# A two-block transformer on one core: gathered rows, gate writes, convolution sums and class values rearranged in a TensorE-bound kernel

## Chip, core and metric

The kernel runs on one core of a Trainium2 chip. The metric is the device time of one execution in microseconds (us); less is better.

## What is computed

The input is one sequence of 512 tokens of 1024 values in fp32. Two blocks follow each other. The parts that the change touches are these, from the reference:

```python
# first block: convolution branch, and the expert layer
glu = zca * jax.nn.sigmoid(zcb)
cv = causal_depthwise_conv(glu, conv_w[l], conv_b[l])            # 31 taps
cv = jax.nn.silu(layer_norm(cv, conv_ln_g[l], conv_ln_b[l]))
y_b = cv @ w_b[l]
...
def block(args):                                                   # 128 experts a token (8 heads x 16)
    hb, eb, gb = args
    act = jax.nn.gelu(jnp.einsum('thkd,td->thk', u_tab[eb], hb), approximate=False)
    return jnp.einsum('thk,thkd->td', gb * act, v_tab[eb])
...
# second block: attention over blocks, and over tokens that lie 4 apart
for (win, dil, nh) in A_GROUPS:                                    # ((128,1,6), (512,4,5), (2048,16,5))
    ...
    v_sel = vg[:, idx]
    o = jnp.einsum('bqhk,bqkhd->bqhd', p.astype(vg.dtype), v_sel)
```

`u_tab` and `v_tab` have 16,384 rows of 1024 values. The second block also has a differential attention and two MLPs, which the change leaves alone.

## The kernel before

Activations lie with features on the 128 partitions and the 512 tokens along the free axis, in eight tiles. Every product is formed from a high and a low part, so each is three matmuls (L121, L122, L123 in `mm3`): high by high, high weight by low activation, low weight by high activation. Weights come as units of 128x1024 fp32 (0.524 MB). `unit` loads one into `raw` over SP's DMA queue (L94; three buffers), ScalarE (ACT) rounds it to `whi` (L103) and VectorE (DVE) makes the rest `wlo` (L104). A raw buffer is free again after L104. In the expert stage a fourth pair of whi and wlo buffers is used. The order of instructions on each engine is set when the kernel is built, by a scheduler that simulates a timeline; on the chip each engine and each DMA queue keeps to that order.

**Convolution sums (`stage_a`).** After the 31 taps the layer norm needs, for each token, the sum over all 1024 channels. The eight tiles `cv` are multiplied by a matrix of ones on TensorE (PE) and accumulated in PSUM (L346), the mean is subtracted (L351, DVE), the squares made on ACT (L353) and summed by eight more matmuls with ones (L354). An fp32 matmul with ones runs as two passes, so the trace has 16 for eight. At the same time the recurrent branch's output `O` is made tile by tile: PE transposes (L339), DVE gates the result (L340), ACT and DVE split it (L112, L113). The gemms with `w_a` consume `O` in the same order, three at a time (one for each of the three PSUM tiles `g`).

**Experts (`stage_p`).** 384 tokens are done densely: a loop of 32 chunks ("u loop") multiplies four units of `peer_u` each by the 384 tokens, applies gelu on ACT (L578) and writes the chunk `at` to DRAM (`act_d`, L579). Beside it `route` builds the gates: for 32 tokens at a time DVE makes one-hot tiles `oj`, `ol`, `oh` (L722 to L725), PE multiplies them (L730, L731), ACT copies the result into `G` (L733, 8 copies, one buffer) and SP writes the 2.1 MB of `G` to `g_d` (L736); that happens 12 times. The second loop of 32 chunks ("v loop") reads `at` back (L588) and the gates `gt` of that chunk (L589), which need all 12 writes; 0.786 MB each. DVE multiplies them to `w` (L591), ACT and DVE split it into `wph` and `wpl` (L112, L113), and PE adds 72 matmuls of 512 columns a chunk to six PSUM accumulators (L601 to L603). `prep(c + 1)` runs a chunk ahead.

The remaining 128 tokens are done by gathering table rows with an indirect DMA from POOL (GpSimd; L649): 128 gathers from `peer_ur` ("dots": DVE multiplies and reduces each, L654), then 128 from `peer_v` ("sums": DVE accumulates into `yt`, L664 and L666). Each gather moves 128 rows, 0.524 MB. Dots and sums form one generator, `gather_steps`, with four buffers `gu`; a call `gather(n)` advances it by n.

**Class values (`attn0`).** For the heads of the dilated groups the values are needed with tokens of one residue modulo 4 together. `vgemm_class` runs `gemm_tok` (L157 to L159) with N = 320 columns of weights moving; the stationary operand is an activation tile of which every fourth token is taken (`CLS`). That is 96 matmuls a call, and two calls. `cls_pv` multiplies the values `vC` with the transposed probabilities (L1065, L1066, L1072).

Of the kernel before, what the change touches and what calls it, by code (L numbers as in the profile page):

```python
# [52 lines left out]
class Kern:  # L53
# [188 lines left out]
    def stage_a(self):  # L242
# [33 lines left out]
        with self.pool("a_sl") as sl, self.pool("a_glu") as gl:  # L276
# [52 lines left out]
            with self.pool("a_tmp") as pt:  # L329
# [25 lines left out]
                va = tmp("mu", 1)  # L355
                nc.scalar.copy(out=va, in_=ps)
                vt = nps("m")
                for b in range(4):
                    nc.tensor.matmul(vt[:, 2 * b:2 * b + 2], va[:, self.BLK[b]], self.ident[:, 0:2], start=True, stop=True)
# [187 lines left out]
    def stage_p(self):  # L547
# [7 lines left out]
        with self.pool("p_gath") as pgt, self.pool("p_wh") as pwh, self.pool("p_wl") as pwl:  # L555
# [6 lines left out]
            steps = self.gather_steps(pgt)  # L562

            def gather(n):
                for _ in range(n):
                    next(steps, None)
            with self.pool("p_at") as pa, self.pool("p_rp", bufs=2, space=PSUM) as pq:
                self.route(pq, X, g_d, gather)
                TD = self.TD
                for c in range(CH):  # L570
                    at = pa.tile([P, 4, TD], F32, tag="at0", name="at0", bufs=2)
                    for i in range(4):
                        hi, lo = self.unit(A["peer_u"][c * 4 + i])
                        ps = self.pg.tile([P, T], F32, tag="g", name="g")[:, 0:TD]
                        for k in range(KD):
                            w = slice(k * P, (k + 1) * P)
                            self.mm3(ps, hi[:, w], lo[:, w], X[0][k][:, P:], X[1][k][:, P:], k == 0, k == KD - 1)
                        nc.scalar.activation(out=at[:, i], in_=ps, func=AF.Gelu)  # L578
                    nc.sync.dma_start(out=act_d[c], in_=at)  # L579
                    gather(1)  # L580
            with self.pool("p2") as pp, self.pool("p2p", space=PSUM) as pv:
                tmp = self.tmpf(pp, 2)
                acc = [self.pg.tile([P, T], F32, tag="g", name="g") if n < 3 else pv.tile([P, T], F32, name=f"ac{n}") for n in range(2 * ND)]

                def prep(c):
                    at = pp.tile([P, 4, TD], F32, tag="at", name="at", bufs=2)
                    gt = pp.tile([P, 4 * ND, 4, 32], F32, tag="gt", name="gt", bufs=2)
                    nc.sync.dma_start(out=at, in_=act_d[c])  # L588
# [15 lines left out]
                Ws = {0: prep(0)}  # L604
                for c in range(CH):
                    if c + 1 < CH:
                        Ws[c + 1] = prep(c + 1)
                    W = Ws.pop(c)
                    if c + 1 < CH:
                        for i in range(4):  # L610
                            hi, lo = self.unit(A["peer_v"][c * 4 + i])
                            for b in range(ND):
                                vmm(b, i, W, hi, lo, c == 0 and i == 0, False)
# [5 lines left out]
                    gather(6)  # L619
                gather(1000)  # L620
# [20 lines left out]
    def gather_steps(self, pool):  # L641


        nc, A = self.nc, self.A
        tabs = A["peer_ur"], A["peer_v"].rearrange("i j d -> (i j) d")

        def rows(tab, s):
            t = pool.tile([P, 1024], F32, tag="gu", name="gu", bufs=4)
            nc.gpsimd.indirect_dma_start(  # L649
                out=t, out_offset=None, in_=tab, in_offset=bass.IndirectOffsetOnAxis(ap=self.eidx[:, s:s + 1], axis=0))  # L650
            return t
        for s in range(P):
            u = rows(tabs[0], s)
# [6 lines left out]
            yield  # L660
        for s in range(P):
            v = rows(tabs[1], s)
# [305 lines left out]
    def attn0(self, X, g):  # L968
        nc, tc, A = self.nc, self.tc, self.A
        with self.pool("at0") as pa, self.pool("at0s") as ps_, self.pool("at0p", space=PSUM) as ppool:  # L970
# [5 lines left out]
            vC = [pa.tile([P, 4, 320], F32, name=f"vC{c}") for c in range(2)]  # L976
# [91 lines left out]
            def cls_pv(pr, po, pTs):  # L1068
                for r in range(4):
                    for hh in range(2):  # L1070
                        i = 2 * pr + hh - 6
                        nc.tensor.matmul(po[64 * hh:64 * hh + 64, self.BLK[r]], vC[i // 5][:, r, (i % 5) * 64:(i % 5) * 64 + 64], pTs[hh][:, self.BLK[r]],  # L1072
                                         start=True, stop=True)
# [8 lines left out]
            vgemm_class(0)  # L1082
            keep = {}
            for pr in range(3, 8):
# [7 lines left out]
                if pr < 5:  # L1092
                    po = pp("O")
# [43 lines left out]
            vgemm_class(1)  # L1137
# [216 lines left out]
def pack(I):  # L1354
# [37 lines left out]
    D["a_v1"] = _tok(w[:, 2432:3072], 320, 2)  # L1392
# [24 lines left out]
```

## Time and profile before

| what | value |
|---|---|
| time, median of 3 runs | 3213.58 us (3207.55 to 3220.32) |
| the profiled execution's own time | 3211.22 us |
| its span, first to last instruction | 3209.4 us |
| PE busy | 3072.0 us, 96% of the span |
| DVE busy | 2239.3 us, 70% |
| ACT busy | 1246.3 us, 39% |
| POOL busy | 420.3 us, 13% |
| DMA | 581.30 MB, mean 181 GB/s |
| mean granted TensorE clock | 0.984 of full speed |

The span runs from the first instruction to the last; the time of an execution is some 2 us longer. Busy times of consecutive matmuls overlap, since they are pipelined, so PE's pace is read as the count of matmuls in a stretch, and its idle time as what is missing from 50 us in a window of 50. A hole in PE's work counts where the last wait in it ends; idle time of another engine counts for nothing by itself.

### The profile page before, as it was taken

Reading aid. Unit: us, or ns where it says so; the run is one execution under the profiler, and the core shown is the slowest. Engines: PE = TensorE matmul, PEld = TensorE weight load, DVE = VectorE, ACT = ScalarE, POOL = GpSimd, SP = SyncE. Lnnn points to the kernel's source line nnn. Section 1 sums busy time; section 2 is a strip of 40 time slices with the busy share of each in tenths; the row PEclk is TensorE's granted clock in tenths of the full one; section 3 lists DMA queues with packets and bytes.
Section 4 is the critical chain, followed back from the end, with each engine's and each line's share of the span. In section 5 each row is a group of like instructions: output and inputs, shape, how many; then the busy total and the mean of one; then the engine's idle time right before and its main releaser. Section 6 shows DMA issues by size and latency. Waiting matters only on the chain.

```text
span 3209.4 us, 40754 instructions
## 1 busy us (share of the span) xinstructions
PE 3072.0 (96%) x15395; PEld 2604.1 (81%) x15395; DVE 2239.3 (70%) x4004; ACT 1246.3 (39%) x1970; POOL 420.3 (13%) x328
## 2 busy tenths in 40 slices
PE   6999999899999999599989999999999999999998
PEld 4788878789999899587777887788888877778886
DVE  7999967699999999787776545445544457554443
ACT  4267762334334343333223334453222245532221
POOL 0000000000333333444441001000000000000000
PEclk9999999999999999799999999999999999999999
DMA  6442227435899899999997642222333333133332
GB/s 220 147 165 70 73 86 234 152 101 158 310 340 357 323 360 345 375 361 354 342 330 265 229 147 88 62 65 81 105 97 94 110 92 96 51 96 97 97 99 72
DMA packets 200548, 581.30 MB, mean 181 GB/s; under 512 B 18368, under 2 KB 72528, under 8 KB 198816
## 3 DMA queue, kind: packets, MB, share of 16 engines
q1 hardware_dynamic: 160144, 432.93, 40.5%
q0 software_dynamic: 39776, 144.97, 12.1%
q8 instruction: 121, 1.98, 0.3%
q10 hardware_dynamic: 432, 0.80, 0.1%
q14 instruction: 75, 0.61, 0.1%
HBM read 526.12 MB, written 63.00 MB: 184 GB/s over the span
## 4 chain that ended last, share of the span: by engine, by line
PE 85%; DMA 6%; DVE 5%; issue 2%; ACT 2%; POOL 0%; DVEq 0%; POOLq 0%; SPq 0%; ACTq 0%
PE g L121 21%; PE g L122 20%; PE g L123 20%; DMA raw<-in_peer_v 4%; PE g L601 2%; PE g L602 2%; PE ac L601 2%; PE ac L602 2%; PE g L603 2%; PE ac L603 2%; PE S L1224 1%; DVE wlo L104 1%; PE L L480 1%; DVE yt L666 1%; PE Gp L730 1%
## 5 line engine op out<-in xcount | busy, mean ns | idle before, releaser
L103 ACT CAST whi<-raw 128x1024 fp32r<-128x1024 f32 (+2 forms) x556 | 577.0, 1045 | 1164.5 <-PE g L122 669.9
L121 PE MATMUL g<-xh,whi 128*128 128x512 f32 (+1 forms) x2368 | 874.0, 371 | 16.8 <-ACT xh L112 8.9
L123 PE MATMUL g<-xh,wlo 128*128 128x512 f32 (+1 forms) x2368 | 872.6, 370 | 6.6 <-DVE wlo L104 6.6
L122 PE MATMUL g<-xl,whi 128*128 128x512 f32 (+1 forms) x2368 | 875.8, 370 | 3.1 <-DVE xl L113 3.1
L104 DVE TENSOR_TENSOR wlo<-raw,whi 128x1024 fp32r<-128x1024 f32 (+2 forms) x556 | 674.5, 1215 | 220.1 <-ACT whi L103 216.6
L121 PEld LDWEIGHTS g<-xh,whi 128*128 128x128 f32 x2368 | 446.9, 189 | 77.3 <-ACT xh L112 9.3
L123 PEld LDWEIGHTS g<-xh,wlo 128*128 128x128 f32 x2368 | 446.6, 189 | 61.6 <-DVE wlo L104 8.1
L122 PEld LDWEIGHTS g<-xl,whi 128*128 128x128 f32 x2368 | 446.9, 189 | 59.8 <-DVE xl L113 5.3
L649 POOL DMA_INDIRECT gu<-in_peer_v,eidx x128 | 202.5, 1582 | 253.8 <-DVE yt L666 220.3
L649 POOL DMA_INDIRECT gu<-in_peer_ur,eidx x128 | 161.7, 1264 | 474.5 <-DVE ga L654 222.0
L601 PE MATMUL g<-whi,wph 128*128 128x512 f32 x384 | 155.4, 406 | 51.8 <-ACT whi L103 28.3
L121 PE MATMUL g<-mh,whi 128*128 128x512 f32 x512 | 199.2, 389 | 0.0
L122 PE MATMUL g<-ml,whi 128*128 128x512 f32 x512 | 199.2, 389 | 0.0
L123 PE MATMUL g<-mh,wlo 128*128 128x512 f32 x512 | 199.2, 389 | 0.0
L188 POOL TENSOR_TENSOR tr_r<-tr_v,mhalf 128x4 f32<-128x4 f32 x15 | 17.3, 1156 | 1281.9 <-DVE tr_v L187 1281.9
L914 DVE TENSOR_TENSOR h<-g,h 128x512 f32<-128x512 f32 x64 | 44.3, 692 | 194.0 <-PE g L123 194.0
L666 DVE SCALAR_TENSOR_TENSOR yt<-gu,ga,yt 128x1024 f32<-128x1024 f32 x127 | 163.1, 1284 | 20.0 <-DMA gu<-in_peer_v,eidx 18.8
L327 DVE SCALAR_TENSOR_TENSOR s<-glu,vec,s 128x512 f32<-128x512 f32 x232 | 164.3, 746 | 0.1
L654 DVE CUSTOM_DVE_ANT_0 gu<-gu,xt 128x1024 f32<-128x1024 f32 x128 | 155.4, 1220 | 6.1 <-DMA gu<-in_peer_ur,eidx 5.9
L602 PE MATMUL g<-whi,wpl 128*128 128x512 f32 x384 | 154.3, 402 | 0.0
L601 PE MATMUL ac<-whi,wph 128*128 128x512 f32 x384 | 153.1, 400 | 0.0
L602 PE MATMUL ac<-whi,wpl 128*128 128x512 f32 x384 | 152.3, 397 | 0.0
(443 smaller groups left out, 4750.8 us busy)
## 6 DMA issues: line engine op xcount, KB each, us to landing
raw<-in_peer_u SPq DMA_DIRECT2D x128, 512.0 KB
raw<-in_peer_v SPq DMA_DIRECT2D x128, 512.0 KB
raw<-in_mlp_in SPq DMA_DIRECT2D x64, 512.0 KB
raw<-in_mlp_out SPq DMA_DIRECT2D x64, 512.0 KB
raw<-in_w_in SPq DMA_DIRECT2D x56, 512.0 KB
act_d<-at SPq DMA_DIRECT2D x32, 768.0 KB
g_d<-G SPq DMA_DIRECT2D x12, 2048.0 KB
at<-act_d SPq DMA_DIRECT2D x32, 768.0 KB
```

Of the source, the lines that this page charges most:

```text
L103: nc.scalar.copy(out=hi[:, :n], in_=raw[:, :n])
L104: nc.vector.tensor_sub(out=lo[:, :n], in0=raw[:, :n], in1=hi[:, :n].bitcast(F32))
L121: nc.tensor.matmul(ps, wh, xh, start=start, stop=False)
L122: nc.tensor.matmul(ps, wh, xl, start=False, stop=False)
L123: nc.tensor.matmul(ps, wl, xh, start=False, stop=stop)
L327: nc.vector.scalar_tensor_tensor(o, glu[n][:, j:j + T], self.v("conv_w", n * 31 + j), acc, ALU.mult, ALU.add)
L601: nc.tensor.matmul(ps, wh[:, i], hi[:, s], start=first, stop=False)
L602: nc.tensor.matmul(ps, wl[:, i], hi[:, s], start=False, stop=False)
L603: nc.tensor.matmul(ps, wh[:, i], lo[:, s], start=False, stop=last)
L649: nc.gpsimd.indirect_dma_start(out=t, out_offset=None, in_=tab, in_offset=bass.IndirectOffsetOnAxis(ap=self.eidx[:, s:s + 1], axis=0))
L654: nc.vector.tensor_tensor_reduce(out=u, in0=u, in1=self.xt, scale=1.0, scalar=0.0, op0=ALU.mult, op1=ALU.add, accum_out=self.ga[:, s:s + 1])
L666: nc.vector.scalar_tensor_tensor(self.yt, v, self.ga[:, s:s + 1], self.yt, ALU.mult, ALU.add)
```

## The change

Four parts. **Gathers:** the generator is split. The dots have a pool of their own during `route` and the u loop and are drained at its end; the sums begin only in the v loop, in its pool, two ahead of the first chunk and then four and five a chunk by turns (six a chunk before, of whichever were left). **Chunk order:** the last u chunk's `at` is not written to DRAM and read back; the v loop begins with it and goes on with 0 to 30. The `at` tiles of both loops come from one pool. **Convolution sums:** DVE adds the eight tiles of `cv`, and one matmul with ones follows; the squares are added on DVE by `sq_add`, and the four small matmuls behind them multiply by ones in place of the identity. **Class values:** `vgemm_class` is called for each pair of heads (`pr` 3 to 7); it runs `gemm_unit` (24 matmuls of 512 columns, weights stationary), copies the result on ACT, transposes the four classes on PE and scales them on DVE into one tile `vC`. The weights are packed as units; their bytes are the same.

```diff
@@ stage_a
-                ps = nps("m")
-                for k in range(KD):
-                    nc.tensor.matmul(ps, self.ones, cv[k], start=(k == 0), stop=(k == KD - 1))
+                cs = tmp("mu", 1)
+                nc.vector.tensor_tensor(cs, cv[0], cv[1], ALU.add)
+                for k in range(2, KD):
+                    nc.vector.tensor_tensor(cs, cs, cv[k], ALU.add)
+                ps = nps("m")
+                nc.tensor.matmul(ps, self.ones, cs, start=True, stop=True)
                 mu = tmp("mu", 1)
                 nc.scalar.activation(out=mu, in_=ps, func=AF.Copy, scale=1.0 / 1024)
-                ps = nps("m")
+                va = tmp("va", 1)
                 for k in range(KD):
                     nc.vector.tensor_sub(cv[k], cv[k], mu)
-                    sq = tmp()
-                    nc.scalar.activation(out=sq, in_=cv[k], func=AF.Square)
-                    nc.tensor.matmul(ps, self.ones, sq, start=(k == 0), stop=(k == KD - 1))
-                va = tmp("mu", 1)
-                nc.scalar.copy(out=va, in_=ps)
+                    self.sq_add(tmp, va, cv[k], k == 0)
@@ stage_p
-            steps = self.gather_steps(pgt)
...
+            with self.pool("p_gu") as pgu, self.pool("p_rp", bufs=2, space=PSUM) as pq:
+                dots = self.gather_dots(pgu)
+                self.route(pq, X, g_d, lambda n: gather(dots, n))
                 for c in range(CH):
...
-                    nc.sync.dma_start(out=act_d[c], in_=at)
-                    gather(1)
+                    if c < CH - 1:
+                        nc.sync.dma_start(out=act_d[c], in_=at)
+                    gather(dots, 3 if c < 16 else 2)
+                gather(dots, 1000)
+                last = at
             with self.pool("p2") as pp, self.pool("p2p", space=PSUM) as pv:
+                sums = self.gather_sums(pp)
+                gather(sums, 2)
...
-                    nc.sync.dma_start(out=at, in_=act_d[c])
+                    if c < CH - 1:
+                        nc.sync.dma_start(out=at, in_=act_d[c])
...
-                for c in range(CH):
+                order = [CH - 1] + list(range(CH - 1))
+                Ws = {0: prep(order[0])}
+                for n, c in enumerate(order):
...
-                    gather(6)
-                gather(1000)
+                    gather(sums, 5 if n % 2 else 4)
+                gather(sums, 1000)
@@ attn0
-            def vgemm_class(c):
-                self.gemm_tok(pp, ("g", "g", "g", "T"), [A["a_v1"][c * 4 + i] for i in range(4)], 320, X,
-                              lambda b, ps: nc.scalar.activation(out=vC[c][:, b], in_=ps, func=AF.Copy, scale=self.rt[:, 4 + b:5 + b]),
-                              lambda b: self.CLS[b])
+            def vgemm_class(pr):
+                ps = self.gemm_unit(A["a_v1"][pr - 3], X)
+                v = tmp()
+                nc.scalar.copy(out=v, in_=ps)
+                tp = pp("T")
+                for r in range(4):
+                    nc.tensor.transpose(tp[:, self.BLK[r]], v[:, self.CLS[r]], self.ident)
+                c = (pr - 3) * P
+                nc.vector.tensor_tensor(
+                    vC[:, :, c:c + P], tp.rearrange("p (r d) -> p r d", r=4), self.rt[:, 4:8].unsqueeze(2).to_broadcast([P, 4, P]), ALU.mult)
...
-            vgemm_class(0)
...
                 if pr < 5:
+                    vgemm_class(pr)
                     po = pp("O")
...
-            vgemm_class(1)
+            for pr in range(5, 8):
+                vgemm_class(pr)
```

How the compiled order moves is shown at three places. Each row has its place on its engine, its line, the operation and the tiles.

First DVE at the convolution sums, where PE waits for DVE to make `O` (L340, then L113). Before:

```order
622 L528 SCALAR_TENSOR_TENSOR s_3010<-s_3010,s_2990,M 128x128 x2
623 L340 SCALAR_TENSOR_TENSOR s_415<-b,vec,s_3513 128x512
624 L340 SCALAR_TENSOR_TENSOR s_416<-b,vec,s_3524 128x512
625 L317 TENSOR_SCALAR ms<-ms 128x4
626 L113 TENSOR_TENSOR s_3521<-s_415,s_3505 128x512
627 L113 TENSOR_TENSOR s_3532<-s_416,s_3506 128x512
628 L320 TENSOR_TENSOR s_422<-s_422,ms 128x512
629 L340 SCALAR_TENSOR_TENSOR s_417<-b,vec,s_3535 128x512
```

After (L346 and L348 are now the adds of `cv`):

```order
622 L528 SCALAR_TENSOR_TENSOR s_3010<-s_3010,s_2990,M 128x128 x2
623 L346 TENSOR_TENSOR mu<-glu_439,glu_440 128x512
624 L348 TENSOR_TENSOR mu<-mu,glu_441 128x512
625 L348 TENSOR_TENSOR mu<-mu,glu_442 128x512
626 L348 TENSOR_TENSOR mu<-mu,glu_443 128x512
627 L340 SCALAR_TENSOR_TENSOR s_415<-b,vec,s_3513 128x512
628 L340 SCALAR_TENSOR_TENSOR s_416<-b,vec,s_3524 128x512
629 L348 TENSOR_TENSOR mu<-mu,glu_444 128x512
630 L317 TENSOR_SCALAR ms<-ms 128x4
631 L340 SCALAR_TENSOR_TENSOR s_417<-b,vec,s_3535 128x512
632 L113 TENSOR_TENSOR s_3521<-s_415,s_3505 128x512
```

Four adds now stand ahead of the first gated tile, and six instructions in place of three lie between its L340 and its L113.

Second SP's DMA queue from the last `peer_u` weights to the first gates read. Before:

```order
184 L736 DMA g_d<-G 128x4096
185 L579 DMA act_d<-at_12079 128x1536
186 L94 DMA raw<-in_peer_v 128x1024 x3
187 L579 DMA act_d<-at_12212 128x1536
188 L94 DMA raw<-in_peer_v 128x1024
189 L736 DMA g_d<-G 128x4096
190 L94 DMA raw<-in_peer_v 128x1024 x2
191 L736 DMA g_d<-G 128x4096
192 L588 DMA at<-act_d 128x1536
193 L589 DMA gt<-g_d 128x12x128
```

After (L749 is the write of `G`, L597 and L598 the reads of `at` and `gt`):

```order
186 L749 DMA g_d<-G 128x4096
187 L94 DMA raw<-in_peer_v 128x1024
188 L583 DMA act_d<-at 128x1536
189 L94 DMA raw<-in_peer_v 128x1024
190 L597 DMA at<-act_d 128x1536
191 L94 DMA raw<-in_peer_v 128x1024 x3
192 L749 DMA g_d<-G 128x4096
193 L94 DMA raw<-in_peer_v 128x1024
194 L749 DMA g_d<-G 128x4096
195 L598 DMA gt<-g_d 128x12x128 x2
```

The last chunk's `act_d` write is gone, the first `gt` follows the last gate write directly, and an `at` read (chunk 0, the second to be summed) has moved ahead of the last two gate writes.

Third DVE around the first `w` of the v loop. Before:

```order
2123 L724 TENSOR_TENSOR oh<-ol,gh 128x2048
2124 L666 SCALAR_TENSOR_TENSOR yt<-gu,ga,yt 128x1024
2125 L725 TENSOR_TENSOR ol<-ol,gl 128x2048
2126 L666 SCALAR_TENSOR_TENSOR yt<-gu,ga,yt 128x1024 x6
2127 L629 TENSOR_TENSOR fm<-vec 128x8
2128 L666 SCALAR_TENSOR_TENSOR yt<-gu,ga,yt 128x1024 x4
2129 L591 TENSOR_TENSOR w<-at,gt 128x12x4x32
2130 L113 TENSOR_TENSOR wpl<-w,wph 128x1536
2131 L591 TENSOR_TENSOR w<-at,gt 128x12x4x32
2132 L666 SCALAR_TENSOR_TENSOR yt<-gu,ga,yt 128x1024 x2
```

After (L600 is `w`; L677 and L679 are the sums):

```order
2115 L104 TENSOR_TENSOR wlo<-raw,whi 128x1024
2116 L738 TENSOR_TENSOR ol<-ol,gl 128x2048
2117 L640 TENSOR_TENSOR fm<-vec 128x8
2118 L600 TENSOR_TENSOR w<-at,gt 128x12x4x32
2119 L113 TENSOR_TENSOR wpl<-w,wph 128x1536
2120 L677 TENSOR_SCALAR yt<-gv,ga 128x1024
2121 L600 TENSOR_TENSOR w<-at,gt 128x12x4x32
2122 L679 SCALAR_TENSOR_TENSOR yt<-gv,ga,yt 128x1024 x2
2123 L113 TENSOR_TENSOR wpl<-w,wph 128x1536
2124 L679 SCALAR_TENSOR_TENSOR yt<-gv,ga,yt 128x1024
```

Of the 128 sums, 27 stood ahead of the first `w`; now none does. Counted along the whole order, 31, 51 and 125 sums stood ahead of the 3rd, 8th and 22nd `w`; now 4, 26 and 127 stand ahead of the 3rd, 8th and 27th. After the last matmul of the u loop PE had 96 gate matmuls (L730, L731) to run before the first of the v loop; now it has 64, those of the last `G` alone, and the others are done 23 u matmuls before the end.

## Rows read from the trace of the kernel before

**Rows 1.** Page, first part: busy time, share of the span, instructions.

```profile
PE 3072.0 (96%) x15395; PEld 2604.1 (81%) x15395; DVE 2239.3 (70%) x4004; ACT 1246.3 (39%) x1970; POOL 420.3 (13%) x328
```

**Rows 2.** Windows: busy us and counts per engine, granted clock, DMA share, GB/s.

```profile
1300.00:1350.00 50.00, 26.30 (x219) 24.88 (x217) 35.86 (x32) 14.95 (x25) 22.10 (x14) 0.76 0.98 378
1350.00:1400.00 50.00, 39.18 (x161) 32.19 (x162) 37.07 (x28) 12.03 (x10) 23.82 (x14) 0.83 1.03 373
...
1650.00:1700.00 50.00, 43.10 (x177) 34.36 (x176) 33.95 (x27) 15.59 (x14) 19.72 (x13) 0.94 0.89 331
...
1750.00:1800.00 50.00, 50.00 (x222) 41.42 (x221) 25.00 (x19) 16.79 (x15) 0.00 (x0) 1.00 0.71 239
```

**Rows 3.** Chain that ended last, 1310 to 1365: start, length, what.

```profile
1321.32 10.48 DMA g_d<-G
1331.91 0.61 ACT G L733
...
1338.08 9.22 DMA g_d<-G
1347.32 10.09 DMA gt<-g_d
1357.50 1.77 DVE w L591
1359.29 1.48 ACT wph L112
1360.82 1.65 PE g L601 x3
```

**Rows 4.** ACT's timeline at the end of the u loop.

```profile
1317.59 0.49 ACT L578 ACTIVATE at<-g 128x384 f32<-128x384 f32 x1 [1.61 <-PE g L123]
```

**Rows 5.** DVE's timeline: the 4th, 8th and 22nd w.

```profile
1384.68 1.75 DVE L591 TENSOR_TENSOR w<-at,gt 128x1536 f32<-128x1536 f32 x1
...
1450.25 1.75 DVE L591 TENSOR_TENSOR w<-at,gt 128x1536 f32<-128x1536 f32 x1
...
1720.18 1.75 DVE L591 TENSOR_TENSOR w<-at,gt 128x1536 f32<-128x1536 f32 x1
```

**Rows 6.** Waits, 1320 to 1930: us in total, times, longest.

```profile
POOL gu L649 <- DVE yt L666: 206.0, 76, 10.8
ACT whi L103 <- DMA raw<-in_peer_v: 145.7, 51, 10.8
```

**Rows 7.** Lines L346 and L354, PE: duration min/median/max, first and last start.

```profile
L346 PE MATMUL m<-glu,ones x16: 590/592/595, 418.7 to 425.2; 128*128 128x512 f32 x16
...
L354 PE MATMUL m<-tmp,ones x16: 590/592/595, 431.7 to 445.0; 128*128 128x512 f32 x16
```

**Rows 8.** Timelines of PE and DVE around the convolution sums.

```profile
425.58 1.04 PE L339 MATMUL b<-ident,s 128*128 128x128 f32 x8
...
418.48 1.41 DVE L340 SCALAR_TENSOR_TENSOR s<-b,vec,s 128x512 f32<-128x512 f32 x2 [1.75 <-PE b L339]
...
421.11 1.29 DVE L113 TENSOR_TENSOR s<-s,s 128x512 fp32r<-128x512 f32 x2 [0.34 <-ACT s L112]
...
426.89 2.49 DVE L351 TENSOR_TENSOR glu<-glu,mu 128x512 f32<-128x512 f32 x4
```

**Rows 9.** PE's timeline in the second class gemm: 24 matmuls apart.

```profile
2138.31 0.39 PE L157 MATMUL g<-whi,xh 128*128 128x320 f32 x1
...
2143.91 0.39 PE L157 MATMUL g<-whi,xh 128*128 128x320 f32 x1
```

**Rows 10.** Lines by form, 2040 to 2200: busy us, mean ns, idle before.

```profile
L1065 PE MATMUL T<-ident,p 128*128 128x128 f32 x40 | 5.6, 274 | 0.0
...
L158 PEld LDWEIGHTS T<-wlo,xh 128*128 128x128 f32 x16 | 5.3, 330 | 0.0
```

**Rows 11.** Page, fifth part: weight loads of the unit gemms.

```profile
L121 PEld LDWEIGHTS g<-xh,whi 128*128 128x128 f32 x2368 | 446.9, 189 | 77.3 <-ACT xh L112 9.3
```

More of the change, by code (lines that the diff above doesn't have):

```diff
@@ L554, in stage_p @@
         g_d = self.dram.tile([4 * ND, P, P, 32], F32, name="g_d")
[L555 removed]
+        with self.pool("p_gath") as pgt, self.pool("p_wh") as pwh, self.pool("p_wl") as pwl, self.pool("p_at") as pa:
             self.wx, self.wn = (pwh, pwl), -1
@@ L561, in stage_p, with gather, atile @@
             self.ga = pgt.tile([P, P], F32, name="ga")
-            steps = self.gather_steps(pgt)
-            def gather(n):
+            def gather(steps, n):
                 for _ in range(n):
                     next(steps, None)
-            with self.pool("p_at") as pa, self.pool("p_rp", bufs=2, space=PSUM) as pq:
-                self.route(pq, X, g_d, gather)
+            def atile():
+                return pa.tile([P, 4, self.TD], F32, tag="at", name="at", bufs=2)
+            with self.pool("p_gu") as pgu, self.pool("p_rp", bufs=2, space=PSUM) as pq:
+                dots = self.gather_dots(pgu)
+                self.route(pq, X, g_d, lambda n: gather(dots, n))
                 TD = self.TD
                 for c in range(CH):
-                    at = pa.tile([P, 4, TD], F32, tag="at0", name="at0", bufs=2)
+                    at = atile()
                     for i in range(4):
@@ L585, in prep @@
                 def prep(c):
-                    at = pp.tile([P, 4, TD], F32, tag="at", name="at", bufs=2)
+                    at = last if c == CH - 1 else atile()
                     gt = pp.tile([P, 4 * ND, 4, 32], F32, tag="gt", name="gt", bufs=2)
-                    nc.sync.dma_start(out=at, in_=act_d[c])
+                    if c < CH - 1:
+                        nc.sync.dma_start(out=at, in_=act_d[c])
                     nc.sync.dma_start(out=gt, in_=g_d[:, :, 4 * c:4 * c + 4, :].rearrange("c j i t -> j c i t"))
@@ L612, in stage_p @@
                             for b in range(ND):
-                                vmm(b, i, W, hi, lo, c == 0 and i == 0, False)
+                                vmm(b, i, W, hi, lo, n == 0 and i == 0, False)
                     else:
@@ L639, in stage_p, with gather_rows, gather_dots @@
         return Xn
[L641 to L651, printed above, removed]
+    def gather_rows(self, t, tab, s):
+        self.nc.gpsimd.indirect_dma_start(
+            out=t, out_offset=None, in_=tab, in_offset=bass.IndirectOffsetOnAxis(ap=self.eidx[:, s:s + 1], axis=0))
+        return t
+    def gather_dots(self, pool):
+        nc = self.nc
         for s in range(P):
-            u = rows(tabs[0], s)
+            u = self.gather_rows(pool.tile([P, 1024], F32, tag="gu", name="gu", bufs=4), self.A["peer_ur"], s)
             nc.vector.tensor_tensor_reduce(
@@ L660, in gather_steps, with gather_sums @@
             yield
+    def gather_sums(self, pool):
+        nc = self.nc
+        tab = self.A["peer_v"].rearrange("i j d -> (i j) d")
         for s in range(P):
-            v = rows(tabs[1], s)
+            v = self.gather_rows(pool.tile([P, 1024], F32, tag="gv", name="gv", bufs=4), tab, s)
             if s == 0:
@@ L975, in attn0 @@
             vN = pa.tile([P, 4, 384], F32, name="vN")
-            vC = [pa.tile([P, 4, 320], F32, name=f"vC{c}") for c in range(2)]
-            def vgemm_class(c):
-                self.gemm_tok(pp, ("g", "g", "g", "T"), [A["a_v1"][c * 4 + i] for i in range(4)], 320, X,
-                              lambda b, ps: nc.scalar.activation(out=vC[c][:, b], in_=ps, func=AF.Copy, scale=self.rt[:, 4 + b:5 + b]),
-                              lambda b: self.CLS[b])
+            vC = pa.tile([P, 4, 640], F32, name="vC")
+            def vgemm_class(pr):
[8 more added lines that the diff above has]
+                    vC[:, :, c:c + P], tp.rearrange("p (r d) -> p r d", r=4), self.rt[:, 4:8].unsqueeze(2).to_broadcast([P, 4, P]), ALU.mult)
             self.gemm_tok(pp, vtags, [A["a_v0"][i] for i in range(4)], 384, X,
```

15 lines of the change are left out of this document (7 added, 8 removed).

## Prediction

> **What bounds the kernel now.** I read the page's busy times first, then the windows of 50 us, then the chain where a window is thin, then single lines. PE is busy for 96% of the span [rows 1]: the reader should expect that only removed PE work, or a hole in PE's work that closes, moves the time. The windows show how PE's pace is read: 222 matmuls of 512 columns in 50 us, 0.225 us each, where nothing disturbs it (the last row of [rows 2]). The one large hole is the border between the two expert loops: 26.30 and 39.18 of 50 us busy, granted clock 0.76 and 0.83. Then comes the v loop: 177 matmuls in 50 us, clock 0.94, where the undisturbed stretch has 222 [rows 2]. In both, the DMA engines are 0.89 to 1.03 busy and move 331 to 378 GB/s; in the last row they have 0.71 and 239, and PE loses nothing. So PE waits for bytes there, and the waits say it: ACT's rounding of `peer_v` weights waits 145.7 us for its loads in 51 waits, while POOL waits 206.0 us for DVE's sums [rows 6], that is, the gathers are issued as fast as sums free their buffers.
>
> **The border.** The last gelu of the u loop is at 1317.59 [rows 4], the first v matmul at 1360.82: 43.2 us. The chain between [rows 3]: a `g_d` write of 10.48 us that the only G buffer waits for, ACT's copies of the last G from 1331.91 to 1338.08 (6.2 us), its write of 9.22, the read `gt` of 10.09, then `w` and its split until PE starts, 3.3. All this goes while gathers of the sums fill the queues; 27 sums precede the first `w`. After, no sum precedes it, the last G but one is ready on PE 23 u matmuls ahead of the end, and only one G is left to build behind it. With its copies done about 3 us before the end the sum after is: write landing, 6.2 of copies, a write, a read, 3.3. With the three transfers as long as now, −3 + 10.5 + 6.2 + 9.2 + 10.1 + 3.3 = 36.3 us: 7 us won. If they take only what their bytes need at the 378 GB/s of the window (2.1, 2.1 and 0.786 MB: 5.5, 5.5, 2.1), 19.6 us: 24 won. The traffic that remains is four weight loads and the prefetched `at`, but a lone write or read has a delay of its own that no row here shows, so I stay nearer the first: **−14** (29 us). The Trainium skill ("DMA: Bandwidth & Descriptors", "Anatomy of one DMA — SWDGE (gpsimd) path") gives a time of about 2.0 us plus the bytes at 436 GB/s for a software-queued transfer; carried over to these three as an estimate, it would make 6.8, 6.8 and 3.8, and the gain 19. That the chunk that comes first needs no `act_d` write and read adds nothing: `at` does not stand in the chain [rows 3]. The u loop also gets its dots in another code order, but the compiled order has the same number of dots by each weight unit, so nothing is booked there.
>
> **The v loop.** From the 4th to the 8th `w` the loop takes (1450.25 − 1384.68)/4 = 16.4 us a chunk, and 72 matmuls at 0.225 need 16.2: nothing lost, with about 4 sums a chunk (20 in 5 chunks). From the 8th to the 22nd it takes (1720.18 − 1450.25)/14 = 19.28, with 74 sums, 5.3 a chunk: 3.07 us lost in each [rows 5], 43 us in all. In bytes this fits: four units 2.1 MB, `at` and `gt` 1.57, and 4 sums 2.1 make 5.77 MB in 16.4 us, 352 GB/s; with 5.3 sums 6.45 MB would need 398 GB/s at PE's pace, more than the 378 that any row here has. The source asks for 4.5 a chunk after, but the compiled order shows what DVE is given: 22 sums from the 3rd to the 8th `w` (4.4 a chunk), then 101 from the 8th to the 27th (5.3). The pace that costs is kept, and 19 chunks run at it in place of 14, since the 27 sums of the border are done here now. 5 × 3.07 = **+15**. Bounds: if each chunk costs only what its bytes need at 378 GB/s, 5.1 sums a chunk from the 3rd to the 27th (6.34 MB, 16.8 us) lose 0.6 × 24 = 14 us where 43 are lost now: −29. If all 26 chunks go at the worst window's pace, 50/177 × 72 = 20.3 us, they lose 4.1 × 26 = 107: +64.
>
> **Convolution sums.** The first 16 passes with ones begin at 418.7 and the next PE work at 425.58: 6.9 us; the second 16 have the same shape and duration [rows 7, 8]. 13.8 us of PE go, 0.9 comes back with the one remaining matmul. But the first 7 us were also cover: PE ran them while DVE and ACT made the first pieces of `O`. DVE now has four adds, at 0.62 us each as L351 [rows 8], ahead of the first gated tile; it sat idle 1.75 there, so that tile is 0.7 late, and the L113 that PE needs comes behind one more add and another gate: about 422.7 in place of 421.8. PE has 1.6 us of its own work until then from 418.7 (transposes of two tiles, three matmuls that need no L113), so about 2.4 us lie open. −13.8 + 0.9 + 2.4 = **−10**. The seven adds of squares follow behind the gate of the last tile and are hidden under the gemms of `w_a`; their result is due five gemms of 5.4 us later, when `w_b` starts. If DVE paces the three gemms to their end, up to 6 more are lost (−4); with nothing open it is −13.
>
> **Class values.** The matmuls of 320 columns follow each other at (2143.91 − 2138.31)/24 = 0.233 us [rows 9], more than the 0.225 of 512 columns. Their weight loads, from every fourth token, take 330 ns [rows 10]; those of the unit gemms 189 [rows 11]. 192 × 0.233 = 44.8 us go. 120 matmuls at 0.225 come, 27.0, and 20 transposes of 0.14 to 0.27 [rows 10], 2.8 to 5.5. PE saves 12 to 15. Copy, transposes and scaling stand in a chain ahead of `cls_pv`, and some of it will lie open at the last pair; I take 3 off: **−11**. The lower bound is −2, if that chain lies open by some 2 us for each of the five pairs (12 − 10).
> Against this stands a rule of the Trainium skill ("TensorE: Matmul & The Clock Gate", "LDWEIGHTS (loading the stationary operand)"): a load takes about a column a cycle at 1.2 GHz and hides behind the matmul before it, so a matmul costs its columns at 2.4 GHz and a few ns. By it 192 of 320 columns take an estimated 26 us, 120 of 512 take 26 with the transposes on top, and the change would lose 3. The trace does not agree with it for strided operands: 0.233 us where it has 0.136.
>
> **Sum.** −14 + 15 − 10 − 11 = −20. The profiled execution took 3211.22, 2.4 below the median of three runs; 3211.2 − 20 = **3191 us**.
>
> **Rivals.** *Main case*, as above: 3191, own range 3179 to 3203; 0.48.
> *A, the loop recovers.* The 3.07 us are the price of a backlog that the border's gathers build up (DMA at 1.03 before the loop has settled [rows 2]); without it the loop is limited by bytes alone. 3211 − 14 − 10 − 11 − 29 = 3147, or 3169 half way. For it: the chunks right behind the border ran at 352 GB/s without loss. Against it: the loss is as large 300 us later. 0.18.
> *B, the other side: slower.* The sums are spread over 26 chunks and each runs at the worst window's 20.3 us: 3211 − 14 − 10 − 11 + 64 = 3240. It decides by the loss in a chunk: the total passes 3214 once 26 chunks lose 3.1 each, and 3230 at 3.7. For it: chunks 4 to 8 lose nothing now and the window at 1650 has 43.10 of 50, so it gets worse while the sums last. Against it: 4.4 sums in the first chunks, which cost nothing now. 0.09.
> *C, a PE saving uncovers DVE.* The sums of `cv` or the class chain pace PE, and one of the two gives nothing: 3201 to 3202. 0.12. In the class part a third way is that the price goes by columns, 0.225 × 320/512 = 0.141 us: 192 cost 27 us, as much as the 120 that replace them, and the transposes are 3 us lost: 3205. Against it stands the row's 0.233. The Trainium skill's section above is this rule. 0.04.
> *D, the border stays.* The transfers are long by themselves, and PE's last gates wait on the single G as before: −6 at most, 3199. 0.09.
>
> **Range and chances.** The range takes in A half way and more, and stops short of B: 3155 to 3215. What a measurement of this kernel can tell from no change is 0.5%, 16 us: below 3197.5 is faster, above 3229.7 slower. Faster: most of the main case, A, a little of D: 0.61. Slower: B: 0.08. Same: 0.31.
>
> **What would show it.** Right: the chain from the last gelu to the first v matmul at 27 to 32 us, with no sum in it; in the v loop about 16.5 us a chunk up to the 8th `w`, then 19 to 19.5 until the 27th, and DMA above 330 GB/s there; no L354, first `w_a` results some 10 us earlier; in `attn0` no weight load of 330 ns in a 320-column gemm. Wrong: chunks that stay near 16.8 with sums running (A), or at 20 from the first on (B); `gt` still 10 us long without gathers (D); PE waiting for L113 or L340 beyond 3 us, or for the scaling of `vC` (C).

## The result, and the profile after

The changed kernel takes 3195.23 us, median of 6 runs (3189.31 to 3207.16), against 3213.06 for the kernel before (6 runs): the ratio is 0.9944, 95% interval 0.992 to 0.9967, 18 us less, where 20 were predicted. In a second group it was 3199.77 (5 runs) against 3214.73 (17 runs), ratio 0.9962 (0.9949 to 0.9974), 12 us less.

The profiled execution is the slowest of the six (3207.16 us), so totals are taken from the runs and only stretches from the profiles. The first line is the span; the second answers to [rows 1].

```profile
span 3205.2 us, 40593 instructions
...
PE 3065.3 (96%) x15313; PEld 2592.2 (81%) x15313; DVE 2249.6 (70%) x4020; ACT 1243.2 (39%) x1963; POOL 415.1 (13%) x328
```

PE has 6.7 us less busy time, as far as overlapping busy times tell.

**The border.** The last gelu in ACT's timeline (first row) and the chain from there to the first v matmul:

```profile
1320.88 0.48 ACT L581 ACTIVATE at<-g 128x384 f32<-128x384 f32 x1
```

```profile
1317.55 8.77 DMA g_d<-G
1326.42 0.60 ACT G L746
...
1333.00 6.27 DMA g_d<-G
1339.34 4.90 DMA gt<-g_d
1344.33 1.77 DVE w L600
1346.12 1.48 ACT wph L112
1347.64 1.65 PE g L610 x3
```

Set beside [rows 3, 4]: the steps are the same and none of their waits has gone, but the first of the three transfers starts 3.3 us ahead of the last gelu, where it started 3.7 us behind it, and the three take 8.77, 6.27 and 4.90 us in place of 10.48, 9.22 and 10.09. The border is 1347.64 − 1320.88 = 26.8 us, 43.2 before; about 7 us of the difference are the earlier start and 10 the shorter transfers. The windows show the traffic that left it, 233 GB/s in place of 378 [rows 2], and that the last sums now weigh on a window that was undisturbed:

```profile
1300.00:1350.00 50.00, 28.61 (x217) 27.11 (x217) 19.77 (x18) 17.34 (x27) 0.00 (x0) 0.79 0.67 233
1350.00:1400.00 50.00, 50.00 (x215) 41.25 (x214) 40.77 (x32) 14.19 (x13) 24.50 (x16) 0.97 1.01 366
...
1750.00:1800.00 50.00, 43.12 (x166) 34.56 (x167) 34.84 (x29) 13.87 (x13) 19.72 (x13) 0.90 0.83 303
```

**The v loop.** The 4th, 8th and 27th `w` on DVE, which answer to [rows 5]:

```profile
1371.45 1.75 DVE L600 TENSOR_TENSOR w<-at,gt 128x1536 f32<-128x1536 f32 x1
...
1438.69 1.75 DVE L600 TENSOR_TENSOR w<-at,gt 128x1536 f32<-128x1536 f32 x1
...
1813.07 1.75 DVE L600 TENSOR_TENSOR w<-at,gt 128x1536 f32<-128x1536 f32 x1
```

(1438.69 − 1371.45)/4 = 16.8 us a chunk, then (1813.07 − 1438.69)/19 = 19.7. The waits of this stretch have the same names as [rows 6], one with more in it:

```profile
ACT whi L103 <- DMA raw<-in_peer_v: 177.8, 62, 10.3
```

These are ACT's waits, however, and not PE's. PE stands still for 38.5 us of the loop, nearly always at an L610 that waits for its `whi` (first row). In nine of these holes the load had landed, eight times 0.7 to 5.9 us before PE ran out of work. But in ACT's compiled order the split `wph` for the next chunk stands ahead of that `whi`, and this split waits until PE has finished the chunk before (`wph` has two buffers). PE then stands still for one `wph` and one `whi`, 2.5 us. The other rows show ACT and then PE at one of the nine; the DMA engines are 0.37 busy from 1472 to 1482:

```profile
PE g L610 <- ACT whi L103: 37.2, 15, 3.8
...
1472.23 1.47 ACT L112 CAST wph<-w 128x1536 fp32r<-128x1536 f32 x1 [12.10 <-PE ac L612]
1473.61 2.94 ACT L103 CAST whi<-raw 128x1024 fp32r<-128x1024 f32 x3
...
1474.70 0.50 PE L610 MATMUL g<-whi,wph 128*128 128x512 f32 x1 [2.51 <-ACT whi L103]
```

The nine holes make 22.6 us, and holes that wait for a load 15.8. The rest of the loss, about 30 us against 32 chunks of 16.32, is a slower pace of the matmuls at a mean granted clock of 0.95. The kernel before has seven such places in its loop, 17.5 of 28.4 us of holes.

**Convolution and class values.** DVE's rows show its order at the products with `w_a`: the eight subtractions L355 wait for the mean, the last gate L340 and its L113 come behind them, and the first product L371 follows at 445.49. PE's row shows how little of this lies open, 0.33 us.

```profile
436.61 4.91 DVE L355 TENSOR_TENSOR glu<-glu,mu 128x512 f32<-128x512 f32 x8 [0.73 <-ACT mu L352]
441.43 0.75 DVE L340 SCALAR_TENSOR_TENSOR s<-b,vec,s 128x512 f32<-128x512 f32 x1
...
443.49 0.68 DVE L113 TENSOR_TENSOR s<-s,s 128x512 fp32r<-128x512 f32 x1
...
445.49 1.28 DVE L371 TENSOR_TENSOR s<-g,gate 128x512 f32<-128x512 f32 x2
...
446.33 0.47 PE L121 MATMUL g<-s,whi 128*128 128x512 f32 x1 [0.33 <-DVE s L371]
```

By form, `attn0` has 20 transposes at 0.17 us each (3.4/20), and DVE's scaling waits 4.7 us in all, nearly all of it for them:

```profile
L1000 DVE TENSOR_TENSOR vC<-T,rt 128x512 f32<-128x512 f32 x5 | 3.4, 689 | 4.7 <-PE T L998 4.5
L998 PE MATMUL T<-ident,tmp 128*128 128x128 f32 x20 | 3.4, 291 | 0.0
```

### The profile page after: what moved, and what is told of

Its sections match the earlier page's. It is cut to its first block, busy times and chain, and to the rows that moved or that the text cites. A ratio compares the mean times of both kernels' runs of the same rounds, so it can differ in the third digit from the quotient of the medians.

```text
span 3205.2 us, 40593 instructions
## 1 busy us (share of the span) xinstructions
PE 3065.3 (96%) x15313; PEld 2592.2 (81%) x15313; DVE 2249.6 (70%) x4020; ACT 1243.2 (39%) x1963; POOL 415.1 (13%) x328
## 3 DMA queue, kind: packets, MB, share of 16 engines
q0 software_dynamic: 39776, 144.97, 12.1%
## 4 chain that ended last, share of the span: by engine, by line
PE 70%; DVE 10%; DMA 9%; issue 6%; ACT 2%; POOL 2%; SPq 0%; POOLq 0%; DVEq 0%; ACTq 0%
PE g L121 17%; PE g L122 17%; PE g L123 17%; DMA gv<-in_peer_v,eidx 3%; DVE wlo L104 2%; DMA raw<-in_peer_v 2%; DMA gu<-in_peer_ur,eidx 2%; DVE gu L662 2%; PE S L1245 1%; PE g L610 1%; PE ac L610 1%; PE g L611 1%; PE g L612 1%; PE ac L611 1%; PE ac L612 1%
## 5 line engine op out<-in xcount | busy, mean ns | idle before, releaser
L103 ACT CAST whi<-raw 128x1024 fp32r<-128x1024 f32 (+1 forms) x553 | 575.8, 1049 | 1203.5 <-PE g L122 667.1
L121 PE MATMUL g<-xh,whi 128*128 128x512 f32 (+1 forms) x2408 | 892.3, 372 | 17.8 <-ACT xh L112 8.9
L123 PE MATMUL g<-xh,wlo 128*128 128x512 f32 (+1 forms) x2408 | 891.4, 371 | 6.6 <-DVE wlo L104 6.6
L122 PE MATMUL g<-xl,whi 128*128 128x512 f32 (+1 forms) x2408 | 894.4, 372 | 3.4 <-DVE xl L113 3.4
L104 DVE TENSOR_TENSOR wlo<-raw,whi 128x1024 fp32r<-128x1024 f32 (+1 forms) x553 | 675.3, 1224 | 194.7 <-ACT whi L103 191.1
L121 PEld LDWEIGHTS g<-xh,whi 128*128 128x128 f32 x2408 | 456.2, 190 | 81.0 <-ACT xh L112 9.4
L123 PEld LDWEIGHTS g<-xh,wlo 128*128 128x128 f32 x2408 | 456.0, 189 | 63.7 <-DVE wlo L104 8.9
L122 PEld LDWEIGHTS g<-xl,whi 128*128 128x128 f32 x2408 | 456.0, 189 | 61.6 <-DVE xl L113 5.6
L653 POOL DMA_INDIRECT gv<-in_peer_v,eidx x128 | 197.0, 1539 | 352.7 <-DVE yt L679 240.7
L610 PE MATMUL g<-whi,wph 128*128 128x512 f32 x384 | 156.1, 408 | 52.6 <-ACT whi L103 37.2
L679 DVE SCALAR_TENSOR_TENSOR yt<-gv,ga,yt 128x1024 f32<-128x1024 f32 x127 | 163.0, 1284 | 11.6 <-DMA gv<-in_peer_v,eidx 10.8
L610 PE MATMUL ac<-whi,wph 128*128 128x512 f32 x384 | 157.5, 411 | 0.0
```

Source lines behind the costliest of these rows:

```text
L103: nc.scalar.copy(out=hi[:, :n], in_=raw[:, :n])
L104: nc.vector.tensor_sub(out=lo[:, :n], in0=raw[:, :n], in1=hi[:, :n].bitcast(F32))
L121: nc.tensor.matmul(ps, wh, xh, start=start, stop=False)
L122: nc.tensor.matmul(ps, wh, xl, start=False, stop=False)
L123: nc.tensor.matmul(ps, wl, xh, start=False, stop=stop)
L610: nc.tensor.matmul(ps, wh[:, i], hi[:, s], start=first, stop=False)
```

## The experiments

Twelve runs were made, in three groups of four (two of them repeat a kernel); each ratio is to the kernel before in the same group. The stretches are read in each profile from the same events: "border" from the last gelu to the first v matmul, "loop" from there to the last v matmul's start, "`attn0`" from the last copy of the v loop's result to the first MLP weight load.

| kernel | median us | ratio (95%) | u loop | border | loop | attn0 |
|---|---|---|---|---|---|---|
| before (profile) | 3213 to 3219 | | 585.5 | 43.2 | 570.3 | 254.7 |
| changed (profile) | 3195.23 | 0.9944 (0.992, 0.9967) | 592.1 | 26.7 | 590.3 | 244.9 |
| changed, again | 3199.77 | 0.9962 (0.9949, 0.9974) | 589.8 | 26.6 | 580.6 | 242.1 |
| conv_only | 3203.08 | 0.9956 (0.9941, 0.9972) | 586.6 | 42.4 | 561.6 | 253.5 |
| class_only | 3203.16 | 0.9953 (0.9935, 0.9971) | 585.8 | 40.7 | 581.3 | 245.1 |
| experts_only | 3217.20 | 0.9997 (0.9986, 1.0008) | 587.5 | 29.9 | 580.7 | 255.6 |
| in_order | 3199.61 | 0.9951 (0.9937, 0.9965) | 589.6 | 26.5 | 595.5 | 244.0 |
| gv6 | 3209.18 | 0.9981 (0.997, 0.9991) | 590.4 | 26.7 | 592.3 | 244.5 |
| gv3 | 3159.49 | 0.9824 (0.9805, 0.9842) | 589.0 | 26.4 | 545.0 | 241.0 |
| gv3, again | 3158.93 | 0.9837 (0.9817, 0.9857) | 589.3 | 26.7 | 545.2 | 242.8 |
| gv3_sq | 3165.05 | 0.9846 (0.9832, 0.986) | 589.3 | 27.5 | 544.1 | 245.8 |
| early16_gv3 | 3172.30 | 0.9863 (0.9846, 0.988) | 586.3 | 33.6 | 551.6 | 246.4 |
| sq_only | 3204.74 | 0.9967 (0.9953, 0.9981) | 586.8 | 41.4 | 561.3 | 253.6 |
| class_blk | 3203.82 | 0.9965 (0.9953, 0.9977) | 586.4 | 42.5 | 575.0 | 242.1 |

**One part at a time.** Three kernels have one part of the diff each: the hunk of `stage_a`, those of `attn0` with the packing, those of `stage_p`.

> Only the convolution sums are changed. If the parts add up (my theory), this part gives -8 to -10 us against before (ratio 0.997), PE reaching the first w_b gemm 8 to 10 us earlier, with 2 to 3 us of PE idle in front of the first w_a matmuls. Rival: the DVE adds pace the gemms and nothing is won (within 3 us of before). Second rival: the later start of the first loads of w_a, 4 us late in the profile of the changed kernel, belongs to this part; then the stage up to the convolution shows the same delay here.

> Only the class values are changed. My theory: -10 to -11 us, and nothing moves ahead of attn0. Rival (price by columns): within 3 us of before, or slower.

> Only the gathers and the chunk order are changed. My theory: the border is 14 to 17 us shorter and the loop 15 to 20 longer, the sum 0 to +5 us against before; the u loop takes as long as before. Rival: the u loop itself is longer by 5 to 7 us, as the one profile of the changed kernel has it, because the denser dots make its weight loads wait; then the part is 5 to 12 us slower than before.

The class part does what was expected in its own stage: `attn0` is 9.6 us shorter, and the order ahead of it is unchanged (its longer loop is that of its profiled execution). The kernel's 15 us are more than that stage gives; the interval, 9 to 21, takes in both. The experts part is even, and by the expected pieces: border −13, loop +10, u loop +2. The convolution part gives 14 us, more than its own stage can hold, and the table shows where: its v loop is 9 us shorter than that of before and 20 shorter than class_only's. Nothing in that loop was edited. But the compiled order of DVE differs there: 29 sums stand ahead of the first `w` in place of 27, and the last of 128 is ahead of the 22nd in place of the 23rd; and ACT's order has six of the places where `wph` holds up `whi` in place of seven. sq_only has the same counts and the same loop (561.3). The three profiles whose loops were compiled as before have 570.3, 581.3 and 575.0. So an edit two stages earlier goes with a loop that is 9 to 20 us shorter, through the scheduler's order; the changed kernel has another loop order and does not have this gift. This would account for the parts alone (−14, −15, −1) not adding up to −18 or −12. It rests on two profiles against three; which difference in the order is the cause was not tried.

**The changed kernel again, and the last chunk.** in_order takes back the chunk that stays in SBUF:

```diff
-                    if c < CH - 1:
-                        nc.sync.dma_start(out=act_d[c], in_=at)
+                    nc.sync.dma_start(out=act_d[c], in_=at)
...
-                order = [CH - 1] + list(range(CH - 1))
+                order = list(range(CH))
```

> The changed kernel once more, beside the others of this group. If the three parts add up as they were timed alone (-14, -15 and -1), -26 to -30 us against before; if a part of what they give alone is lost when they stand together, -18 again. Its v loop, first v matmul to last, should take 574 to 584 us, 10 to 20 more than in the orders with the old gathers (555, 564, 575 in three profiles).

> The changed kernel without the part on the last chunk: all 32 chunks are written to DRAM and read back, and the v loop goes from 0 to 31. My theory (the gates' writes and read make the border, not the activations): within 5 us of the changed kernel, border 26 to 30 us from the last gelu to the first v matmul. Rival: the chunk that stays in SBUF is what shortens the border; then it goes back to 33 to 43 us and the kernel is 7 to 15 us slower.

The parts do not add: −12, not −26 to −30. And the chunk order adds nothing: 3199.61 against 3199.77, border 26.5 against 26.6. The rival falls; the last chunk's activations are no part of the border.

**How many sums a chunk.** The number of buffers for the gathered rows is the only edit; the compiled order follows it.

```diff
-            v = self.gather_rows(pool.tile([P, 1024], F32, tag="gv", name="gv", bufs=4), tab, s)
+            v = self.gather_rows(pool.tile([P, 1024], F32, tag="gv", name="gv", bufs=3), tab, s)
```

> The changed kernel with three buffers for the gathered rows of the sums in place of four. The compiled order then has 3.7 sums a chunk in place of 5.3 (104 by the 31st w), and 19 are left behind the last w. If bytes in flight set the loss (my theory: 3.7 sums a chunk are 5.6 MB, 342 GB/s at PE's pace), the loop runs at 16.2 to 16.8 us a chunk, some 55 to 60 us are won in it, and 25 to 65 come back behind its end, where the last sums lie open: 3135 to 3200 us. Rival: each sum costs PE 0.6 us wherever it runs (its descriptors or its DVE work); then the loop stays at 18 us a chunk or more and the whole is slower than the changed kernel by 20 us or more.

> The changed kernel with six buffers for the gathered rows of the sums. The compiled order has 7.4 sums a chunk and all 128 by the 20th w. If bytes set the loss (7.5 MB a chunk, 465 GB/s at PE's pace, against 350 that are moved): 21 to 22 us a chunk from the 4th to the 20th, 5 lost in each, about 80 us in all, 15 to 25 us slower than the changed kernel. Rival (each sum costs PE the same 0.6 us wherever it is): the same time as the changed kernel within 5 us.

The 8th and 20th `w` with three buffers, and then with six:

```profile
1431.64 1.76 DVE L600 TENSOR_TENSOR w<-at,gt 128x1536 f32<-128x1536 f32 x1
...
1639.23 1.76 DVE L600 TENSOR_TENSOR w<-at,gt 128x1536 f32<-128x1536 f32 x1
```

```profile
1448.86 1.75 DVE L600 TENSOR_TENSOR w<-at,gt 128x1536 f32<-128x1536 f32 x1
...
1699.96 1.75 DVE L600 TENSOR_TENSOR w<-at,gt 128x1536 f32<-128x1536 f32 x1
```

Between the 8th and the 20th `w` DVE makes 48, 64 and 90 sums with three, four and six buffers: 4.0, 5.3 and 7.5 a chunk. (The expectation for gv3 had 3.7 and 19 sums behind the last `w`; the trace has 114 sums ahead of the 31st `w` and 9 behind the last.) The chunks take 17.3, 18.8 to 19.2 and 20.9 us, and 16.3 with none (the last chunks of every profile in which the sums end early). The first 4.0 sums cost 0.25 us each, those beyond about 1 us each: (20.9 − 17.3)/3.5 = 1.03. A constant price of 0.6 a sum, the rival, is out. A fixed ceiling of bytes is not right either: 5.8, 6.5 and 7.6 MB a chunk are 333, 340 and 363 GB/s, so the rate still rises while PE already waits. Over the whole loop the kernel with three buffers (first row) even moves more bytes a second than the changed kernel (second row), and PE stands still for 12.1 us in place of 38.5:

```profile
1343.61:1888.59 544.98, 532.86 (x2303) 435.55 (x2304) 409.40 (x320) 178.93 (x161) 206.77 (x125) 0.99 0.90 327
...
1347.64:1937.95 590.31, 551.81 (x2306) 448.21 (x2306) 411.23 (x320) 176.04 (x161) 191.02 (x124) 0.95 0.83 301
```

ACT's order differs too: with three buffers `wph` stands ahead of the `whi` that PE needs at 2 chunks, in place of 9. Over all fourteen profiles the loop goes with the number of these places: 544 to 552 us with 2 (the four with three buffers), 561 to 562 with 6 (conv_only, sq_only), 570 to 581 with 7 (before, class_only, class_blk, experts_only), 581 to 596 with 9 (the changed kernel twice, in_order, gv6). The number of buffers changes the sums a chunk and this order together, so these runs do not tell what each is worth; a kernel with the same sums and `whi` ahead of `wph` was not tried. What is shown is that three buffers give a loop 36 to 45 us shorter than the changed kernel's, less than the 55 to 60 expected, and that the 9 sums behind the last `w` cost nothing that shows, where 25 to 65 us were expected behind the loop: the last of them starts 14.6 us ahead of the last v matmul. With six buffers the total is 9 us more than the changed kernel's, less than the 15 to 25 expected and more than the rival's 5.

**Sums ahead of the border.** 16 sums go in the dots' buffers ahead of the loop, the rest with three:

```diff
+                sums = self.gather_sums(pgu, 'gu', 0, 16)
+                gather(sums, 1000)
                 last = at
...
-                sums = self.gather_sums(pp)
+                sums = self.gather_sums(pp, 'gv', 16, P, 3)
```

> The changed kernel, with the first 16 sums in the dots' buffers before the border and the rest with three buffers: 16 sums stand ahead of the first w, then 3.7 a chunk up to the 31st. By bytes the u loop's end has room (301 GB/s from 1250 to 1300 in the changed kernel) and the loop has the same pace as with three buffers: the same time as with three buffers within 8 us, about 3155, or up to 8 less where the last 19 sums had lain open. Rival: gathers that still run at the border bring its old length back (+8 to +14 us against three buffers).

The time is the rival's: the border is 33.6 us and the loop 551.6, both some 7 longer than with three buffers alone; by the ratios the kernel is 8 to 13 us slower. Its reason is not. No gather is issued between 1318.5 and the first v matmul, and the three transfers are as short as the changed kernel's:

```profile
1316.31 0.48 ACT at L581
...
1320.75 8.02 DMA g_d<-G
...
1335.28 6.26 DMA g_d<-G
1341.68 4.89 DMA gt<-g_d
```

What came back is the old order of the gates: PE has 96 gate matmuls behind the u loop in place of 64, and the first of the three writes starts 4.4 us behind the last gelu in place of 3.3 us ahead of it. Some 3 us of this are moved and not lost, since the u loop is shorter (586.3 us for 589.0). Why the loop is longer, with 16 sums fewer in it, is not shown.

**The sums of the convolution, by halves.** sq_only is the kernel before with the edit on the squares alone (`sq_add`, the matmul with ones behind it); gv3_sq is gv3 with the mean's sums back on PE.

> The kernel before with the squares alone summed on DVE; the sums for the mean stay eight matmuls with ones. If these are cover while DVE makes the first tiles of O (my theory), this half gives its full 6.9 us: from the first transpose L339 to the last w_a product 56 to 57 us in place of 63.1, and the other half in the changed kernel gives only 0 to 2. Rival: both halves give half, 59 to 60 us here.

> The changed kernel with three buffers for the sums, once more, beside the next one: 3155 to 3165 us, 1.6 to 1.9% under before; v loop 540 to 555 us.

> The same with three buffers, and with the mean's sums on PE as before. If the mean's matmuls only fill PE's wait for O, within 3 us of the one with three buffers; by the rival (each half gives half) 4 us slower.

From the first L339 to the last product with `w_a`, the stretch is 63.1 us in each of before, class_only and experts_only, 55.4 to 56.1 with both halves on DVE, 58.6 in sq_only, 57.2 in gv3_sq. So the squares give 4.5 to 5.9 and the mean 1.4 to 3.2: sq_only is nearer the rival, half and half, and gv3_sq nearer my theory, so neither is decided. gv3_sq has a median 6 us above gv3's in the same group, but the intervals of the ratios overlap and the scheduler gave its loop another order, so their times decide nothing either. The row of the eight products in sq_only:

```profile
L367 DVE TENSOR_TENSOR s<-g,gate x8: 680/688/692, 453.2 to 483.2; 128x512 f32<-128x512 f32 x8
```

**What the stride costs.** The class gemms of the kernel before, with neighbouring tokens stationary:

```diff
-                              lambda b: self.CLS[b])
+                              lambda b: self.BLK[b])
```

> The kernel before, in which the class gemms take 128 neighbouring tokens as their stationary operand in place of every fourth (so the values that they make belong to other tokens; same count and shapes of instructions). If the strided weight loads of 330 ns set the pace of 0.233 us (my theory), the loads fall to 189 ns and the matmuls of 320 columns follow each other at 0.19 us or less: 192 x 0.04 = 8 us less in attn0. The Trainium skill's rule (TensorE: Matmul & The Clock Gate, LDWEIGHTS) gives an estimated 0.136 us then, 18 less. Rival: the pace stays at 0.23 and something else than the stride sets it.

PE's timeline, nine matmuls apart, and the weight loads of the same gemm (busy us, mean ns), against 330 in [rows 10]:

```profile
2130.68 0.31 PE L157 MATMUL g<-whi,xh 128*128 128x320 f32 x1
...
2132.00 0.31 PE L157 MATMUL g<-whi,xh 128*128 128x320 f32 x1
```

```profile
L159 PEld LDWEIGHTS g<-whi,xl 128*128 128x128 f32 x30 | 5.6, 188 | 0.0
```

The loads fall to 188 ns and the matmuls follow each other at (2132.00 − 2130.68)/9 = 0.147 us, where they had 0.233 [rows 9]; `attn0` is 12.6 us shorter and the kernel 11 us (0.35%). The stride made the price of 0.233: with it gone, the 320 columns cost 0.147, near the 0.141 that the rival of the prediction had, and a load of 188 ns is no floor for the pace, as I had expected it to be. Both paces are at a granted clock of 1.00. From 2145.7 us, after PE had been idle for 2.0 us, the granted clock is 0.50; there the contiguous loads take 330 ns too and the matmuls follow each other at 0.267 us:

```profile
2145.70:2150.40 4.70, 4.70 (x19) 4.70 (x19) 2.05 (x10) 2.60 (x4) 0.00 (x0) 0.50 0.03 7
```

So loads are to be compared at one clock. The Trainium skill offers a reason for the stride's price in "SBUF — State Buffer", "Door 1: The DMA port swizzle (why `[64,N]` ≈ `[32,N]`)": SBUF is read in lines of 16 bytes, full pace needs two hits in a line, and every fourth fp32 value is one hit in each. The loads of 330 and 188 ns agree with it; the reason itself is not shown by these runs.

## Why the prediction was right, and where it was off

- **Class values (−11): right, in size and reason.** `attn0` is 241.0 to 246.4 us with the new gemms (nine profiles), 253.5 to 255.6 with the old ones: −10 to −11. The stride as the cause was argued from two rows and is now shown by class_blk.
- **The border (−14): right.** 26.5 to 26.7 us in three profiles of the changed order, 40.7 to 43.2 in five with the old gathers: −15. The step went as booked, with shorter transfers and one G less. early16_gv3 separates the two: with the short transfers and the old order of the gates the border is 33.6, so the order gives some 7 us, as booked, and the transfers 7 to 10. What I did not book is that this G's gate matmuls didn't vanish: 32 of them, 0.11 us each in the chain, now run in the u loop (3.5 us), and the u loop is 4 to 6 us longer in the three profiles (585.5 to 586.8 with the old gathers, 589.6 to 592.1). Where fewer were moved it goes the same way: experts_only leaves 80 behind the u loop and has 587.5 and a border of 29.9, early16_gv3 leaves all 96 and has 586.3.
- **The v loop (+15): right in size, its reason half right.** 580.6 to 595.5 us in three profiles (mean 588.8) against 575.5 in the three of the unchanged loop order: +13. The compiled pace of 5.3 a chunk, kept for 19 chunks, is what the runs have, and the chunks up to the 8th cost little, as forecast. But the reason, that PE waits for bytes, covers less than half of PE's holes: the 145.7 us of [rows 6] are ACT's waits, and 22.6 of PE's 38.5 us are the places where `wph` stands ahead of `whi` in ACT's order. The term came out because a loss read in 14 chunks was carried over to 19 of the same kind (seven such places in the former, nine in the latter), whatever made it. Rival A (3147), the loop limited by bytes alone, is out for this order. gv3 comes near it (3159), but by another order of the loop and at 17.3 us a chunk, so it does not show A's mechanism.
- **Convolution sums (−10): too large.** Locally the stretch from L339 to the `w_out` loads is 132 to 133 us in place of 141.1, so −8.6. The first product comes at 444.1 to 447.1 us in place of 449.3 to 452.4, some 5 earlier and not 10. The cover was about right: in four profiles read for it (conv_only, both of the changed kernel, gv3) PE's holes in the stretch are 1.1 to 2.3 us in all, where 2.4 were booked. The larger miss lies ahead of the stretch. In the profiles with this edit L339 also starts later: 421.6 to 424.8 us, in place of 417.8 to 420.9 without, although DVE, PE and ACT have the same order up to there. SP's order differs, and in eight of these ten profiles ACT waits 6 to 7 us for one load of `w_in`; of the two without that wait one has 421.6, the other 423.6. So the cause is not settled. What arrives at the u loop's start is −5.
- **The sum.** By stretches, changed against before: −5 up to the u loop, +4.6 in it, −15.5, +13.3, −10.6: −13, where the runs have −12 and −18. The predicted −20 was 2 to 8 too much: the convolution was booked 5 too high and the u loop 4.6 too low, and the border and the loop came out 1 to 2 better each. That the total is as near as this owes something to these errors running against each other.
- **The other side.** Rival B (3240) asked for 20.3 us in all 26 chunks; the chunks had 16.8 and 19.7. Rival D asked for a `gt` that stays 10 us long without gathers; it took 4.90. Rival C asked for PE waits of over 3 us for L113 or L340, or for the scaling of `vC`; there is none.

The profile showed the border, the pace of the chunks and the price of the class gemms ahead of time, and PE's own waits in the loop, which the prediction did not read. What it could not show is what the recompiled order does elsewhere, such as the loop of conv_only.

## What to carry to other kernels

Gathers beside a weight stream cost little at 4.0 a chunk here and about 1 us each beyond, so their pace should be set where the compiled order obeys: the number of buffers did, and the count in the source did not. Read the waits of the engine that bounds the kernel, not those of its suppliers: here more than half of PE's holes came from one ACT instruction that waits in order, ahead of the one that PE needed. Read the compiled order of every stage after an edit in one stage, since a scheduler with a simulated timeline may move work two stages on by more than the edit is worth. A strided stationary operand can cost more than the matmul; take the stride in a few transposes of the result.

## What the runs showed of the hardware

- At a granted clock of 1.00, weight loads from fp32 values 16 bytes apart take 330 ns, contiguous ones 188, and the matmuls of 320 columns behind them follow each other at 0.233 and 0.147 us. Both are shorter than the load's own duration in the trace, so that duration is no price by itself. At 0.50, contiguous loads take 330 ns as well.
- A `g_d` write of 2.1 MB takes 6.24 to 6.27 us with nothing beside it, 8.02 to 8.77 beside weight loads without gathers, and 9.22 to 10.48 with gathers as well; the read `gt` of 0.786 MB takes 4.75 to 4.90 without gathers and 10.09 beside them and a read of `at`.
